# Value products of all attention heads in one run behind the last transpose, and tiles padded to 512 bytes

## The chip, the cores and the metric

The kernel runs on one core of a Trainium2 chip. The metric is the device time of one execution in microseconds (us), here as the median of several runs. TensorE (PE) multiplies matrices, VectorE (DVE) and ScalarE (ACT) work element by element, GpSimd (POOL) does small copies and memsets, and SyncE (SP) issues nearly all DMAs.

## The reference

A sequence of 512 tokens of width 1024 passes through two blocks, all in float32. The first block has two layers. Each layer runs two kinds of attention side by side, gates both and adds their output projection to x:

```
a = mla_attention(c_q, c_kv, k_r, ...) * silu(gate_a)      # 8 heads, all 512 keys, values 64 wide
b = dilated_attention(dil_qkv, ...) * silu(gate_b)         # 8 heads, 3 dilations, banded, mixed by their lse
x = x + concatenate([a, b], axis=-1) @ w_out[layer]
```

The second block has one layer: a SwiGLU FFN (2816 wide), a mixer, and a second FFN. The mixer adds two gated branches, a linear recurrent unit (RG-LRU) and a sliding-window attention with sinks and a relative bias (16 query heads, 4 key/value heads, 64 wide, windows of three chunks of 64).

In every attention the probabilities are normalised before they meet the values: o = (e / l) @ v.

## The kernel before, in words

**Products.** Activations stand transposed in SBUF, features on the partitions and the 512 tokens along the row. A projection keeps float32 precision by splitting each operand in a rounded high and a low part and taking three products (`mm3`, lines 131 to 133); for a width of 1024 a projection of 128 outputs is 24 products of 512 columns. `weights` loads one 128x1024 tile of weights, ACT writes its high part (`wh`) and DVE the low part (`wl`). These tiles come from the pools in `self.wps`, taken in turn: three times `wp`, and from the first FFN on one buffer of a pool `wx` besides.

**PSUM.** Its eight banks of 512 columns are given out in rings by purpose: `mm` for projections, `s` for scores, `t` for transposes, `o` for attention outputs.

**Order.** The kernel is written for a planner: each instruction has its place in the program as its priority, and the planner simulates the engines and gives each engine, which executes in order, the ready instruction of highest priority. So projections that stand later in the program fill the time in which attention waits for DVE and ACT. A dependency of the kind ORDER fixes only the order of two instructions on the same engine, without a semaphore; `begin` and `behind` make such dependencies.

**Latent attention** (`mla_attend`, 2 layers x 4 pairs of heads). For each of four query tiles r and two heads h: scores (lines 532 to 534), maximum, exponential, normalisation, four transposes into a `t` bank (`turn`, line 549), and one ACT copy of them to `PT` (line 550). `values(r)` then takes the eight products of the tile (line 558): the stationary operand is 64 columns of V, head 0 writes partitions 0 to 63 of the bank `o` and head 1 the other 64. Each such float32 product shows as two instructions in the trace. The loop calls `values(r)` two steps behind the transposes of the tile:

```
for i in range(8 + 1 + 2):
    ...
    i -= 1 + 2
    if i >= 0 and i % 2 == 1:
        values(i // 2)
```

**Dilated attention** (`dil_attend`, 2 layers x 4 pairs). The scores of all eight (tile, head) come first, then the factors that mix the dilations (lines 735 to 743). Then, tile by tile, DVE scales p (line 751), PE transposes (line 753), ACT copies (line 754), and eight products of the values follow (line 700, called through `add`).

**Sliding window** (`swa`, `swa_tile`, 4 groups of 4 query tiles). One call of `swa_tile` makes scores, softmax, transposes (line 1064), copies to `swPT` (three buffers, line 1066), the value products of the tile into half of bank 7 (line 1072: 4 instructions for the first tile, 8 for the others, each over 256 columns), and splits the output in high and low parts.

**Tiles.** Pools are laid out one behind the other in each partition of SBUF. `const` holds the vectors (178 columns, 712 bytes), the identity and a tile of ones; `wp`, `rows`, `xu` (x), `tmp`, `sm` (small vectors) follow, then the pools of the stages.

Of the kernel before, what the change touches and what calls it, by code (L numbers as in the profile page):

```python
# [11 lines left out]
F32 = mybir.dt.float32  # L12
# [10 lines left out]
P = 128  # L23
# [5 lines left out]
EPS = 1e-6  # L29
NEG = -1e30  # L30
GELU_C = 0.7978845608028654
SWAP32 = [i + 16 if i < 16 else i - 16 for i in range(32)]
SWAP16 = [i + 8 if i < 8 else i - 8 if i < 16 else i for i in range(32)]
WIN = (0, 16, 48, 64)
# [8 lines left out]
class Kern:  # L43
    def __init__(self, ctx, tc, a, out):
# [22 lines left out]
        self.ones = self.const.tile([P, P], F32, name="ones")  # L67
        nc.vector.memset(self.ones, 1.0)


    def banks(self, **kinds):

# [10 lines left out]
    def behind(self, ins, first):  # L83

        if first is None:
            return ins
        self.tc.add_manual_dep(ins, first.name, ORDER, reason="the bank's first product")
        return first

    def begin(self, ins, key, start):  # L90
# [233 lines left out]
class Block1:  # L324
# [195 lines left out]
    def mla_attend(self, L, pr, proj):  # L520
        k, nc, ap = self.k, self.k.nc, self.ap
        ve, mm = nc.vector, nc.tensor.matmul
        Q, Kh, Kl = proj
        V = self.VM[pr // 2]
        o = k.bank("o")
        ps, PT = [None] * 8, [None] * 4

        def softmax(r, h):
            c = slice(r * P, (r + 1) * P)
            qh, ql = Q[h]  # L530
            s = k.bank("s")
            mm(s, lhsT=qh[0:96, c], rhs=Kh[0:96, h, :], start=True, stop=False)  # L532
            mm(s, lhsT=qh[0:96, c], rhs=Kl[0:96, h, :], start=False, stop=False)  # L533
            mm(s, lhsT=ql[0:96, c], rhs=Kh[0:96, h, :], start=False, stop=True)  # L534
            mx, nm, l, rl = (k.small(n) for n in ("mx", "nm", "l", "rl"))
            ve.reduce_max(mx, s, axis=AX)
            ve.tensor_mul(nm, mx, self.msc[:, 4 + r:5 + r])
            p = ap.tile([P, S], F32, tag="p", name="p", bufs=8)
            nc.scalar.activation(p, s, AF.Exp, bias=nm, scale=self.msc[:, r:r + 1], accum_out=l)
            ve.reciprocal(rl, l)  # L540
            ve.tensor_scalar(p, p, rl, None, op0=ALU.mult)
            ps[2 * r + h] = p

        def turn(r, h):
            if h == 0:
                PT[r] = ap.tile([P, 2, 4, P], F32, tag="PT", name="PT", bufs=4)
            p, t = ps[2 * r + h], k.bank("t")
            for j in range(4):
                nc.tensor.transpose(t[:, j * P:(j + 1) * P], p[:, j * P:(j + 1) * P], k.ident)  # L549
            nc.scalar.copy(PT[r][:, h], t.rearrange("p (j q) -> p j q", j=4))  # L550

        def values(r):
            c = slice(r * P, (r + 1) * P)
            for j in range(4):
                for h in range(2):
                    vc = (j % 2) * 256 + (pr % 2) * P + 64 * h
                    b = slice(64 * h, 64 * h + 64)
                    k.begin(mm(o[b, c], lhsT=V[j // 2][:, vc:vc + 64], rhs=PT[r][:, h, j], start=j == 0, stop=j == 3),  # L558
                            (o.offset, h), j == 0)

        for i in range(8 + 1 + 2):
            if i < 8:
                softmax(i // 2, i % 2)
            if 0 <= i - 1 < 8:
                turn((i - 1) // 2, (i - 1) % 2)
            i -= 1 + 2
            if i >= 0 and i % 2 == 1:
                values(i // 2)
        self.gated(o, pr)

    def first_values(self, L):
# [119 lines left out]
    def dil_attend(self, L, pr, proj, V):  # L691
# [6 lines left out]
        def add(h, out, v, tile, pt, stop):  # L698
            vc = (tile % 2) * 256 + (pr % 2) * P + 64 * h
            ins = inst(mm(out[64 * h:64 * h + 64], lhsT=V[v][tile // 2][:, vc:vc + 64], rhs=pt,  # L700
                          start=(first[h] is None), stop=stop, skip_group_check=True))
            first[h] = k.behind(ins, first[h])


        own, oth, ps = k.small("own", 32, 2), k.small("oth", 32, 2), []
# [36 lines left out]
        ve.reciprocal(f, f)  # L742
        ve.tensor_mul(f, f, ev[:, 0])
        ov = by_tau(o)
        for n in range(4):
            PT = ap.tile([P, 2, 4, P], F32, tag="PT", name="PT", bufs=4)
            for h in range(2):
                p, t = ps[2 * n + h], k.bank("t")
                for i in range(2):
                    d = slice(256 * i, 256 * i + 256)  # L750
                    ve.tensor_scalar(p[:, d], p[:, d], fv[:, i, n, h:h + 1], None, op0=ALU.mult)
                for j in range(4):
                    nc.tensor.transpose(t[:, j * P:(j + 1) * P], p[:, j * P:(j + 1) * P], k.ident)  # L753
                nc.scalar.copy(PT[:, h], t.rearrange("p (j q) -> p j q", j=4))
            for j in range(4):
                for h in range(2):
                    if j < 2:
                        add(h, ov[:, n], 0, 2 * n + j, PT[:, h, j], False)
                    else:
                        add(h, o[:, n * P:(n + 1) * P], j - 1, n, PT[:, h, j], n == 3 and j == 3)  # L760
# [141 lines left out]
def mixer(k, acc, lead, hd, after, srcs):  # L902
# [3 lines left out]
    k.banks(mm=free[:2], t=(5, 6))  # L906
    rstd, R, first = k.start(acc, lead)
    with k.tc.tile_pool(name="mix", bufs=16, reuse_waits="tile") as mp:
        hb = mp.tile([P, 16], F32, name="hbg", bufs=1)
        o = a["voff"]["b_gate"]  # L910
        ve.tensor_scalar(hb, k.vecs[:, o:o + 16], 0.5, None, op0=ALU.mult)
        G = [None] * 16
# [42 lines left out]
def swa(k, R, rstd, at, gate, first):  # L955
    nc, a = k.nc, k.a
    ve, mm = nc.vector, nc.tensor.matmul
    with k.tc.tile_pool(name="swa", bufs=1, reuse_waits="tile") as sp:
# [38 lines left out]
        keys(0)  # L997
        Q = queries(0)
        keys(1)
        k.banks(mm=(0, 1, 2), s=(3, 4), t=(5, 6), o=(7,))  # L1000

        for g in range(4):
            bias = sp.tile([P, 4, 256], F32, tag="bias", name="bias", bufs=2)
            src = k.biases[4 * g:4 * g + 4]
            nc.sync.dma_start(bias, bass.AP(tensor=src.tensor, offset=src.offset + 127,
                                            ap=[[383, P], [384 * P, 4], [1, 256]]))
            nc.gpsimd.memset(bias[0:64, :, 192:256], NEG)
            nc.gpsimd.memset(bias[64:128, :, 0:64], NEG)
            for T in range(4):
                swa_tile(k, sp, g, T, Q, Kh[g], Kl[g], V, bias, at)  # L1010
            if g < 3:
                Q = queries(g + 1)
            for i in range(4):
                gate(4 * g + i)
# [12 lines left out]
    nc.sync.dma_start(k.biases, fb[0:16, None, :].to_broadcast([16, P, 384]))  # L1027


def swa_tile(k, sp, g, T, Q, Kh, Kl, V, bias, at):  # L1030

    nc = k.nc
    ve, mm = nc.vector, nc.tensor.matmul
# [3 lines left out]
    nk = len(kts)  # L1037
    n = nk * P
    kc = slice(base * P, base * P + 256)
    PT = sp.tile([P, 2, 4, P], F32, tag="swPT", name="swPT", bufs=3)  # L1040
    for hp in range(2):
        t = k.bank("t").rearrange("p (a b c) -> p a b c", a=2, b=2)
        s = k.bank("s", (2, 256))
        mx, nm, l, rl, es = (k.small(x, 2) for x in ("mx", "nm", "l", "rl", "es"))
        sk = k.vecs[:, k.a["voff"]["sinks"] + 4 * g + 2 * hp:][:, 0:2]
        p = sp.tile([P, 2, 256], F32, tag="swp", name="swp", bufs=2)
        for j in range(2):
            hl = 2 * hp + j
            mm(s[:, j], lhsT=Q[hl][:, c], rhs=Kh[:, kc], start=True, stop=False)
            mm(s[:, j], lhsT=Q[hl][:, c], rhs=Kl[:, kc], start=False, stop=True)  # L1050
            ve.tensor_tensor_reduce(out=p[:, j, 0:n], in0=s[:, j, 0:n], in1=bias[:, hl, 256 - n:256], scale=1.0,
                                    scalar=-3e38, op0=ALU.add, op1=ALU.max, accum_out=mx[:, j:j + 1])
        ve.tensor_tensor(mx, mx, sk, op=ALU.max)
        ve.tensor_scalar(nm, mx, -1.0, None, op0=ALU.mult)
        ve.tensor_sub(es, sk, mx)
        for j in range(2):
            nc.scalar.activation(p[:, j, 0:n], p[:, j, 0:n], AF.Exp, bias=nm[:, j:j + 1], accum_out=l[:, j:j + 1])
        nc.scalar.activation(es, es, AF.Exp)
        ve.tensor_add(l, l, es)
        ve.reciprocal(rl, l)  # L1060
        for j in range(2):
            ve.tensor_scalar(p[:, j, 0:n], p[:, j, 0:n], rl[:, j:j + 1], None, op0=ALU.mult)
            for i in range(nk):
                nc.tensor.transpose(t[:, i, j, :], p[:, j, i * P:(i + 1) * P], k.ident)
        for i in range(nk):
            nc.scalar.copy(PT[:, i, 2 * hp:2 * hp + 2, :], t[:, i])

    o = k.bank("o")[:, 0:256]
    for i, kt in enumerate(kts):
        pp = PT[:, i].rearrange("p (a b) q -> p b a q", b=2)  # L1070
        for j in range(2):
            mm(o[64 * j:64 * j + 64, :], lhsT=V[:, kt, g * 64:g * 64 + 64], rhs=pp[:, j], start=i == 0, stop=kt == T)
    for j in range(2):
        k.split(at[0][2 * g + j][:, c], at[1][2 * g + j][:, c], o[:, j * P:(j + 1) * P])


def lru(k, R, lr, other):
# [77 lines left out]
def tile_kernel(ctx, tc, a, out):  # L1155
# [21 lines left out]
                k.take_x(m, x, k.vcol(g, m), acc, part, sq)  # L1177
        return after

    k.wps = [*k.wps, ctx.enter_context(tc.tile_pool(name="wx", bufs=1))]  # L1180
    acc = ffn(k, *acc, 1, hd[0], to(hd[1], "mix_pre_g"), (a["w_k"][0], a["w_k"][1], a["w_q"][0], a["w_q"][1]))
    acc = mixer(k, *acc, hd[1], to(hd[2], "ffn2_pre_g"), up(2))
    ffn(k, *acc, 2, hd[2], to(out, None), ())
# [133 lines left out]
```

## Time and profile before

| | us |
|---|---|
| median of 3 runs | 2182.97 |
| lowest, highest | 2180.61, 2182.98 |
| profiled execution, its own time | 2184.09 |
| its span, first to last instruction | 2182.3 |
| PE busy in the span | 2145.0 |
| DVE, ACT, POOL busy | 1329.7, 965.1, 94.5 |

The profiled execution is one run more. Its span leaves out what lies before the first and behind the last instruction. Busy time of PE is modelled: a matmul is drawn from its start to the modelled end of its results, so that neighbours overlap.

### The profile page before, as it was taken

The numbers are of one execution on the slowest core, as the hardware profiler recorded it, in microseconds if no ns is written. First come the engines' busy times: TensorE is split into PE (matmuls) and PEld (weight loads), VectorE is DVE, ScalarE is ACT, GpSimd is POOL, SyncE is SP. The second block draws the span as 40 slices with busy tenths as digits, with TensorE's granted clock in tenths as the row PEclk, the third lists the DMA queues.
The fourth block names the chain that finished last, engine by engine and source line by source line (L and its number), as shares of the span: only waits on it lengthen the run. The fifth ranks groups of instructions, "written<-read, shape, count | busy, mean of one in ns | idle before, by whom it ended". The sixth has DMA issues, their size and how long they took to land.

```text
span 2182.3 us, 30506 instructions
## 1 busy us (share of the span) xinstructions
PE 2145.0 (98%) x11650; PEld 1773.3 (81%) x11650; DVE 1329.7 (61%) x2958; ACT 965.1 (44%) x1747; POOL 94.5 (4%) x350
## 2 busy tenths in 40 slices
PE   8999999999999999999999999999999999999997
PEld 7778779778788779778888888877788888888886
DVE  5866773765766773868555424966688748555323
ACT  5654443453653443545222223665567535222221
POOL 0000210100000210100000000000000000000001
PEclk9999999999999999999999999999999999999998
DMA  5313223383223333325223323322122425232221
GB/s 168 93 54 91 84 88 125 101 164 106 76 60 91 87 88 116 107 78 174 97 97 97 97 96 102 121 87 69 64 94 95 146 93 168 97 97 97 97 97 58
DMA packets 84690, 219.11 MB, mean 100 GB/s; under 512 B 9632, under 2 KB 29888, under 8 KB 84544
## 3 DMA queue, kind: packets, MB, share of 16 engines
q1 hardware_dynamic: 84544, 217.17, 32.4%
q8 instruction: 91, 1.49, 0.3%
q14 instruction: 55, 0.45, 0.1%
HBM read 190.92 MB, written 15.73 MB: 95 GB/s over the span
## 4 chain that ended last, share of the span: by engine, by line
PE 89%; DVE 5%; ACT 3%; DMA 2%; POOL 1%; issue 1%; SPq 0%; ACTq 0%; DVEq 0%
PE ps L131 24%; PE ps L132 24%; PE ps L133 24%; PE ps L157 4%; PE ps L700 2%; PE ps L558 2%; PE ps L753 2%; PE ps L549 1%; DVE wl L124 1%; POOL oth L645 1%; PE ps L716 1%; PE ps L532 1%; PE ps L534 1%; ACT p L724 1%; PE ps L533 1%
## 5 line engine op out<-in xcount | busy, mean ns | idle before, releaser
L122 ACT CAST wh<-wr 128x1024 fp32r<-128x1024 f32 (+3 forms) x338 | 342.7, 1015 | 735.5 <-PE ps L132 621.2
L131 PE MATMUL ps<-xh,wh 128*128 128x512 f32 x1496 | 589.5, 394 | 0.0
L132 PE MATMUL ps<-xl,wh 128*128 128x512 f32 x1496 | 589.0, 394 | 0.0
L133 PE MATMUL ps<-xh,wl 128*128 128x512 f32 x1496 | 588.8, 394 | 0.0
L124 DVE TENSOR_TENSOR wl<-wr,wh 128x1024 fp32r<-128x1024 f32 (+3 forms) x338 | 398.3, 1180 | 298.2 <-ACT wh L122 295.9
L133 PEld LDWEIGHTS ps<-xh,wl 128*128 128x128 f32 x1496 | 281.2, 188 | 59.0 <-issue 2.5
L131 PEld LDWEIGHTS ps<-xh,wh 128*128 128x128 f32 x1496 | 281.3, 188 | 58.8 <-issue 2.4
L132 PEld LDWEIGHTS ps<-xl,wh 128*128 128x128 f32 x1496 | 281.3, 188 | 57.0 <-issue 1.4
L131 PE MATMUL ps<-gh,wh 128*128 128x512 f32 (+1 forms) x540 | 199.8, 370 | 0.8 <-ACT wh L122 0.6
L132 PE MATMUL ps<-gl,wh 128*128 128x512 f32 (+1 forms) x540 | 199.0, 369 | 1.1 <-DVE gl L171 1.1
L133 PE MATMUL ps<-gh,wl 128*128 128x512 f32 (+1 forms) x540 | 197.5, 366 | 1.2 <-DVE wl L124 1.2
L133 PE MATMUL ps<-wh,xl 128*128 128x256 f32 (+1 forms) x416 | 119.3, 287 | 0.0
L132 PE MATMUL ps<-wl,xh 128*128 128x256 f32 (+1 forms) x416 | 119.3, 287 | 0.0
L131 PE MATMUL ps<-wh,xh 128*128 128x256 f32 (+1 forms) x416 | 118.9, 286 | 0.0
L131 PEld LDWEIGHTS ps<-gh,wh 128*128 128x128 f32 x540 | 101.5, 188 | 20.4 <-ACT wh L122 2.1
L133 PEld LDWEIGHTS ps<-gh,wl 128*128 128x128 f32 x540 | 101.5, 188 | 19.3 <-DVE wl L124 2.5
L132 PEld LDWEIGHTS ps<-gl,wh 128*128 128x128 f32 x540 | 101.6, 188 | 18.8 <-DVE gl L171 2.5
L853 DVE TENSOR_TENSOR x<-ps,R 128x512 f32<-128x512 f32 x44 | 30.4, 691 | 103.9 <-PE ps L133 103.9
L851 DVE TENSOR_TENSOR x<-ps,R 128x512 f32<-128x512 f32 x44 | 30.4, 691 | 85.8 <-PE ps L133 83.8
L132 PEld LDWEIGHTS ps<-wl,xh 128*128 128x128 f32 x416 | 79.4, 191 | 1.5 <-issue 1.0
L645 POOL COPY oth<-own 32x4 f32<-32x4 f32 x256 | 61.2, 239 | 442.1 <-ACT p L724 432.9
L133 PEld LDWEIGHTS ps<-wh,xl 128*128 128x128 f32 x416 | 79.4, 191 | 1.1 <-issue 1.0
(300 smaller groups left out, 3325.2 us busy)
## 6 DMA issues: line engine op xcount, KB each, us to landing
wr<-in_ffn_w SPq DMA_DIRECT2D x132, 512.0 KB, 3.5
wr<-in_w_dqk SPq DMA_DIRECT2D x48, 512.0 KB, 3.6
wr<-in_w_dv SPq DMA_DIRECT2D x20, 512.0 KB, 3.7
wr<-in_w_out SPq DMA_DIRECT2D x16, 512.0 KB, 3.6
wr<-in_w_bgate SPq DMA_DIRECT2D x16, 512.0 KB, 3.5
hd<-h SPq DMA_DIRECT2D x48, 128.0 KB, 1.8
h<-hd SPq DMA_DIRECT2D x24, 256.0 KB, 5.3
wr<-in_w_lat SPq DMA_DIRECT2D x10, 512.0 KB, 4.3
```

The lines of the kernel that those rows point to most:

```text
L122: nc.scalar.copy(hi[:, :cols], w[:, :cols])
L124: nc.vector.tensor_sub(lo[:, :cols], w[:, :cols], hi[:, :cols].bitcast(F32))
L131: first = mm(out, lhsT=wh, rhs=xh, start=start, stop=False)
L132: mm(out, lhsT=wh, rhs=xl, start=False, stop=False)
L133: return first, mm(out, lhsT=wl, rhs=xh, start=False, stop=stop)
L157: self.begin(mm(ps[:, part], lhsT=w[i][:, c], rhs=x[kt][:, part], start=start, stop=kt == KT - 1 and x is self.xl), ps.offset, start)
L558: k.begin(mm(o[b, c], lhsT=V[j // 2][:, vc:vc + 64], rhs=PT[r][:, h, j], start=j == 0, stop=j == 3), (o.offset, h), j == 0)
L645: self.mover.tensor_copy(dst[32 * b:32 * b + 32, a:a + 1], src[32 * a:32 * a + 32, b:b + 1])
L700: ins = inst(mm(out[64 * h:64 * h + 64], lhsT=V[v][tile // 2][:, vc:vc + 64], rhs=pt, start=(first[h] is None), stop=stop, skip_group_chec ...
L753: nc.tensor.transpose(t[:, j * P:(j + 1) * P], p[:, j * P:(j + 1) * P], k.ident)
L851: nc.vector.tensor_mul(x1, ps1, R)
L853: nc.vector.tensor_mul(x3, ps3, R)
```

## The change

In all three attentions the value products are issued behind the last transpose of their pair of heads (latent, dilated) or of their group (sliding window), and ORDER dependencies hold them there. In the sliding window, `swa_tile` now returns the turned weights, and a new function `swa_values` takes the products of four tiles and then splits the outputs. For that `swPT` has four buffers instead of three, the ring `o` two banks instead of one, and `mm` two instead of three.

Besides, unused tiles are added behind the tiles of `const` (160 bytes) and `sm` (448 bytes), and one small tile of the mixer is made 512 bytes wide; with `W_AT = 0` the other calls of `pad` add nothing. All pools then begin at multiples of 512 bytes.

```diff
+W_AT = 0
...
+        self.pad(self.const, 160 + W_AT)
+        self.pad(self.rows, 512 - W_AT)
+        self.pad(self.sm, 448)
+
+
+    def pad(self, pool, size):
+
+        if size % 512:
+            pool.tile([P, size // 4], F32, name="pad", tag="pad", bufs=1)
...
-                nc.tensor.transpose(t[:, j * P:(j + 1) * P], p[:, j * P:(j + 1) * P], k.ident)
+                turned[0] = inst(nc.tensor.transpose(t[:, j * P:(j + 1) * P], p[:, j * P:(j + 1) * P], k.ident))
...
-                    k.begin(mm(o[b, c], lhsT=V[j // 2][:, vc:vc + 64], rhs=PT[r][:, h, j], start=j == 0, stop=j == 3),
-                            (o.offset, h), j == 0)
-
-        for i in range(8 + 1 + 2):
+                    ins = mm(o[b, c], lhsT=V[j // 2][:, vc:vc + 64], rhs=PT[r][:, h, j], start=j == 0, stop=j == 3)
+                    k.begin(ins, (o.offset, h), j == 0)
+                    k.behind(inst(ins), turned[0])
+
+        for i in range(8 + 1):
             if i < 8:
                 softmax(i // 2, i % 2)
-            if 0 <= i - 1 < 8:
+            if i >= 1:
                 turn((i - 1) // 2, (i - 1) % 2)
-            i -= 1 + 2
-            if i >= 0 and i % 2 == 1:
-                values(i // 2)
+        for r in range(4):
+            values(r)
         self.gated(o, pr)
...
             first[h] = k.behind(ins, first[h])
+            k.behind(ins, turned)
...
-        for n in range(4):
-            PT = ap.tile([P, 2, 4, P], F32, tag="PT", name="PT", bufs=4)
+        PTs = [ap.tile([P, 2, 4, P], F32, tag="PT", name="PT", bufs=4) for n in range(4)]
+        for n, PT in enumerate(PTs):
...
+        for n, PT in enumerate(PTs):
             for j in range(4):
...
-        hb = mp.tile([P, 16], F32, name="hbg", bufs=1)
+        hb = mp.tile([P, P], F32, name="hbg", bufs=1)[:, 0:16]
...
-        k.banks(mm=(0, 1, 2), s=(3, 4), t=(5, 6), o=(7,))
+        k.banks(mm=(0, 1), s=(3, 4), t=(5, 6), o=(2, 7))
...
-            for T in range(4):
-                swa_tile(k, sp, g, T, Q, Kh[g], Kl[g], V, bias, at)
+            PTs = [swa_tile(k, sp, g, T, Q, Kh[g], Kl[g], bias) for T in range(4)]
+            swa_values(k, g, PTs, V, at)
...
-    PT = sp.tile([P, 2, 4, P], F32, tag="swPT", name="swPT", bufs=3)
+    PT = sp.tile([P, 2, 4, P], F32, tag="swPT", name="swPT", bufs=4)
...
+def swa_values(k, g, PTs, V, at):
+
+    mm = k.nc.tensor.matmul
+    os = [k.bank("o", (2, 256)) for _ in range(2)]
+    for T, (PT, _) in enumerate(PTs):
+        o = os[T // 2][:, T % 2]
+        kts = range(max(T - 1, 0), T + 1)
+        for i, kt in enumerate(kts):
+            pp = PT[:, i].rearrange("p (a b) q -> p b a q", b=2)
+            for j in range(2):
+                ins = mm(o[64 * j:64 * j + 64, :], lhsT=V[:, kt, g * 64:g * 64 + 64], rhs=pp[:, j], start=i == 0, stop=kt == T)
+                k.begin(ins, (os[T // 2].offset, j), i == 0)
+                k.behind(inst(ins), PTs[3][1])
+    for T in range(4):
+        c = slice(T * P, (T + 1) * P)
         for j in range(2):
...
+            k.split(at[0][2 * g + j][:, c], at[1][2 * g + j][:, c], os[T // 2][:, T % 2, j * P:(j + 1) * P])
```

## Rows read from the trace of the kernel before

**Rows 1.** The page: engines' busy time, and PE's granted clock in 40 slices.

```profile
PE 2145.0 (98%) x11650; PEld 1773.3 (81%) x11650; DVE 1329.7 (61%) x2958; ACT 965.1 (44%) x1747; POOL 94.5 (4%) x350
...
PEclk9999999999999999999999999999999999999998
```

**Rows 2.** The page: the chain that ended last, by engine.

```profile
PE 89%; DVE 5%; ACT 3%; DMA 2%; POOL 1%; issue 1%; SPq 0%; ACTq 0%; DVEq 0%
```

**Rows 3.** Timeline of PE, dilated stage: start us, us, engine, line, operands, count.

```profile
262.33 0.43 PE L700 MATMUL ps<-PT,V 128*64 128x128 f32 x2
262.70 0.50 PE L133 MATMUL ps<-xh,wl 128*128 128x512 f32 x1
263.03 0.39 PE L131 MATMUL ps<-xh,wh 128*128 128x512 f32 x1
263.26 0.40 PE L132 MATMUL ps<-xl,wh 128*128 128x512 f32 x1
263.59 1.09 PE L700 MATMUL ps<-PT,V 128*64 128x128 f32 x14
264.61 0.50 PE L133 MATMUL ps<-xh,wl 128*128 128x512 f32 x1
264.94 0.39 PE L131 MATMUL ps<-xh,wh 128*128 128x512 f32 x1
```

**Rows 4.** Timeline of PE: transposes in three stages, and a visit between them.

```profile
139.69 0.60 PE L549 MATMUL ps<-ident,p 128*128 128x128 f32 x4
...
257.59 0.66 PE L753 MATMUL ps<-ident,p 128*128 128x128 f32 x4
258.18 1.09 PE L700 MATMUL ps<-PT,V 128*64 128x128 f32 x14
259.19 0.66 PE L753 MATMUL ps<-ident,p 128*128 128x128 f32 x4
...
1405.69 0.27 PE L1064 MATMUL ps<-ident,swp 128*128 128x128 f32 x1
```

**Rows 5.** Timeline of PE, sliding-window stage.

```profile
1413.99 0.40 PE L133 MATMUL ps<-xh,wl 128*128 128x512 f32 x1
1414.31 1.08 PE L1072 MATMUL ps<-swPT,swV 128*64 128x256 f32 x8
...
1415.55 0.28 PE L1050 MATMUL ps<-swKl,swQ 128*128 128x256 f32 x1
```

**Rows 6.** Timeline of PE: first and last row of value products.

```profile
81.88 0.43 PE L558 MATMUL ps<-PT,VM 128*64 128x128 f32 x2
...
1560.39 1.08 PE L1072 MATMUL ps<-swPT,swV 128*64 128x256 f32 x8
```

**Rows 7.** Timeline of DVE and ACT in front of the dilated transposes.

```profile
252.89 4.30 DVE L751 TENSOR_SCALAR p<-p,f 128x256 f32<-128x256 f32 x16
...
254.03 1.26 ACT L754 COPY PT<-ps 128x512 f32<-128x512 f32 x2 [0.90 <-PE ps L753]
```

**Rows 8.** Waits of PE: us in total, times, longest.

```profile
PE ps L753 <- DVE p L751: 7.4, 8, 1.2
```

**Rows 9.** Windows, first latent pair and sliding window: busy us, clock, DMA.

```profile
77.00:98.00 21.00, 21.00 (x141) 15.20 (x140) 16.57 (x43) 14.41 (x30) 0.00 (x0) 1.00 0.14 39
...
1393.00:1430.00 37.00, 35.75 (x191) 26.60 (x191) 32.63 (x117) 27.86 (x80) 0.62 (x2) 1.00 0.28 86
```

**Rows 10.** Timeline of PE, first FFN: 24 products, then 72, first and last.

```profile
1017.61 0.40 PE L131 MATMUL ps<-xh,wh 128*128 128x512 f32 x1
...
1022.98 0.39 PE L133 MATMUL ps<-xh,wl 128*128 128x512 f32 x1
1023.21 0.39 PE L131 MATMUL ps<-xh,wh 128*128 128x512 f32 x1
...
1039.33 0.39 PE L133 MATMUL ps<-xh,wl 128*128 128x512 f32 x1
```

**Rows 11.** The page: line, engine, shapes, count, busy us, mean ns, idle before.

```profile
L131 PE MATMUL ps<-xh,wh 128*128 128x512 f32 x1496 | 589.5, 394 | 0.0
```

More of the change, by code (lines that the diff above doesn't have):

```diff
@@ L86, in behind @@
             return ins
-        self.tc.add_manual_dep(ins, first.name, ORDER, reason="the bank's first product")
+        self.tc.add_manual_dep(ins, first.name, ORDER, reason="behind it")
         return first
@@ L525, in mla_attend @@
         o = k.bank("o")
-        ps, PT = [None] * 8, [None] * 4
+        ps, PT, turned = [None] * 8, [None] * 4, [None]
         def softmax(r, h):
@@ L752, in dil_attend @@
                 for j in range(4):
-                    nc.tensor.transpose(t[:, j * P:(j + 1) * P], p[:, j * P:(j + 1) * P], k.ident)
+                    turned = inst(nc.tensor.transpose(t[:, j * P:(j + 1) * P], p[:, j * P:(j + 1) * P], k.ident))
                 nc.scalar.copy(PT[:, h], t.rearrange("p (j q) -> p j q", j=4))
+        for n, PT in enumerate(PTs):
             for j in range(4):
@@ L1027, in rel_biases, with swa_tile @@
     nc.sync.dma_start(k.biases, fb[0:16, None, :].to_broadcast([16, P, 384]))
-def swa_tile(k, sp, g, T, Q, Kh, Kl, V, bias, at):
+def swa_tile(k, sp, g, T, Q, Kh, Kl, bias):
     nc = k.nc
@@ L1063, in swa_tile @@
             for i in range(nk):
-                nc.tensor.transpose(t[:, i, j, :], p[:, j, i * P:(i + 1) * P], k.ident)
+                turned = inst(nc.tensor.transpose(t[:, i, j, :], p[:, j, i * P:(i + 1) * P], k.ident))
         for i in range(nk):
             nc.scalar.copy(PT[:, i, 2 * hp:2 * hp + 2, :], t[:, i])
-    o = k.bank("o")[:, 0:256]
-    for i, kt in enumerate(kts):
-        pp = PT[:, i].rearrange("p (a b) q -> p b a q", b=2)
+    return PT, turned
+def swa_values(k, g, PTs, V, at):
[12 more added lines that the diff above has]
+        c = slice(T * P, (T + 1) * P)
         for j in range(2):
-            mm(o[64 * j:64 * j + 64, :], lhsT=V[:, kt, g * 64:g * 64 + 64], rhs=pp[:, j], start=i == 0, stop=kt == T)
-    for j in range(2):
-        k.split(at[0][2 * g + j][:, c], at[1][2 * g + j][:, c], o[:, j * P:(j + 1) * P])
+            k.split(at[0][2 * g + j][:, c], at[1][2 * g + j][:, c], os[T // 2][:, T % 2, j * P:(j + 1) * P])
 def lru(k, R, lr, other):
@@ L1178, in to @@
         return after
-    k.wps = [*k.wps, ctx.enter_context(tc.tile_pool(name="wx", bufs=1))]
+    wx = ctx.enter_context(tc.tile_pool(name="wx", bufs=1))
+    k.wps = [*k.wps, wx]
+    k.pad(wx, W_AT)
+    if W_AT:
+        k.pad(ctx.enter_context(tc.tile_pool(name="wy", bufs=1)), 512 - W_AT)
     acc = ffn(k, *acc, 1, hd[0], to(hd[1], "mix_pre_g"), (a["w_k"][0], a["w_k"][1], a["w_q"][0], a["w_q"][1]))
```

## The prediction

> **What bounds the kernel now.** I read the page first. [...] "Busy" is not the whole reading, because ends of matmuls are modelled. What counts is the pitch, the time from one start to the next, and for this the timeline of PE alone is the view to read.
>
> There the reader should look at what happens where a value product (128x64 stationary, so half of the array's columns) stands next to anything that uses all 128 columns. Undisturbed 512-column products follow each other in 0.23 us (263.03 to 263.26). A visit of 14 value instructions lasts 1.02 us to the next start, one of 2 lasts 0.37 us, so twelve more cost 0.65 us, 0.054 us each [rows 3]. Now measure across a visit: from the product at 263.26 to the second one behind the visit at 264.94 are 1.68 us. In it are two full products (0.46) and 14 value instructions (0.76), together 1.22. So 0.46 us are spent on nothing but going into the narrow form and coming back. Between transposes it is a little less: transposes stand 0.11 us apart (four take 0.60, one alone 0.27, and the difference is three pitches), and 257.59 to 259.19 are 1.60 us for four of them (0.44) and 14 value instructions (0.76), which leaves 0.40 [rows 4]. In the sliding-window stage, 1413.99 to 1415.55 are 1.56 us for one 512-column product (0.23), eight value instructions of twice the columns (0.87 at twice 0.054) and one 256-column score product (0.12, half of a 512-column one), which leaves 0.34 [rows 5].
>
> How many visits there are is counted as rows of that timeline with line 558, 700 or 1072 between other rows: 66, 64 and 16, 146 in all, the first at 81.88 and the last at 1560.39 [rows 6]. 48 of those of line 700 stand between transposes on both sides. They are so many because the first product of a tile needs only head 0's copy and the rest also needs head 1's, so that the order on PE is 2, something else, 14.
>
> **The change, part by part.** *Value products behind the last transpose.* No product, transpose, copy or DMA is added or removed. Removed are entries and exits. Now: 48 x 0.40 + 82 x 0.46 + 16 x 0.34 = 19.2 + 37.7 + 5.4 = 62.3 us. After: one visit for each of 8 pairs of the latent stage, 8 pairs of the dilated stage and 4 groups of the window stage, 16 x 0.46 + 4 x 0.34 = 8.7 us. That is 53.6 us less, all on PE, the engine that sets the end. The value instructions themselves keep their 0.054 us.
>
> Is the run really unbroken? Its last quarter needs the copy of the last transposes. A copy is issued about 0.63 us after the one before it (two in 1.26) [rows 7]. Three quarters of a pair's run, 48 instructions, take 2.6 us, so that this copy has landed well before it is needed; I cost that wait at nothing. Without that cover it would be one copy, 0.6 us, in 20 places, 12 us. Were the planner to cut each pair's run once, 16 more visits would cost 7.4 us.
>
> *What takes the place of the value products among the transposes.* In the dilated stage a pair has 8 blocks of transposes, 3.5 us of PE. They are paced by DVE's scaling of p (16 in 4.30 us, 0.54 a block) and ACT's copies (0.63 a block, 5.0 us for 8) [rows 7]. Today value products fill the difference of 1.5 us. Later only projections of the next pair can. If they do, nothing is lost; if none does, 8 x 1.5 = 12 us. PE already waits in front of these blocks for DVE's p, 7.4 us in 8 places [rows 8], so the planner's idea of DVE is too rosy there. I take 4 us lost, nearer to full cover, since one 512-column product of 0.23 us fits each hole.
>
> *Four buffers for the turned weights at once* (window stage, from three) and all four of a dilated pair allocated ahead: the values that free them come before the next pair's transposes in the program, so nothing waits; cost nothing. The output evacuation (`gated`, `keep`, the splits) comes after the run, a few us later than for the first tile now; behind it lie the next projections. *Projection banks in the window stage fall from three to two* (bank 2 now holds outputs). One projection of 24 products takes 5.5 us (24 at 0.23), the bank behind it has that long to be read; DVE is busy 32.63 of 37 us there and PE idle 1.25 [rows 9]. I cost it at nothing, with 4 groups x 1 us as the upper bound.
>
> *Padding.* The pads put every pool at a multiple of 512 bytes. Before, the program places the weight buffers of pool `wp` and x at 352 beyond such a multiple, block-1 tiles, hidden rows and the weight buffer of pool `wx` at 416, mixer tiles at 480; the sizes of the pads undo just these (160 = 512 - 352; with 160 and 448, 416 becomes 1024). Does placement show? Yes: 24 products of one projection whose weights lie in `wx` start at 1017.61 and end their starts at 1022.98, 23 pitches of 233.5 ns; the next 72, weights and x both at 352, run from 1023.21 to 1039.33, 71 pitches of 227.0 ns [rows 10]. From the FFN on every fourth weight tile lies in `wx`; about 26 projections of x, 630 products, have the former placement, and at 6.5 ns each they give 4.1 us. Other pairings I leave at nothing, with plus or minus 4 us. [...]
>
> **Sum.** The profiled execution took 2184.09 us, 1.1 above the median shown, 2182.97. 2184.1 - 53.6 + 4 - 4.1 = 2130.4, and on the scale of the median 2129.
>
> **Rivals.** (a) *PE starves a little or the runs are cut*: full 12 us in the dilated blocks and 7.4 us of cuts, 2129 + 8 + 7 = 2144, up to 2165. For it: the waits of [rows 8]. Against: the many projections that follow at once.
>
> (b) *Placement is worth more.* Everything that PE reads lies today at an odd multiple of 32 bytes, so a true multiple of 64 or 512 was never seen. If it took another 6.5 ns off each of the 3 x 1,496 products of lines 131 to 133 that read x [rows 11], that is 29 us: 2100. For it: one placement step does cost that much. Against: nothing in the trace shows a pitch far below 227. [...]
>
> (c) *Slower: the attention stretches are paced by DVE and ACT, not by PE.* Then they keep their length when value products leave, PE idles there, and the runs are added behind: 16 x (64 x 0.054 + 0.46) = 63 us and some 13 for the window groups, 2184 + 76 = 2260 at worst. It decides from 3.4 us of new idle time a pair (53.6 / 16). For it: DVE 16.57 of 21 us busy in the first latent pair, 32.63 of 37 in the window stage [rows 9]. Against: PE is busy for all of the 21 us in that stretch, and the projections that now follow as a block can move in.
>
> (d) *The change does little*: other matmuls interleave with the run wherever the planner likes, and only placement remains, about 2179.
>
> **How the numbers follow.** Forecast, 2115 to 2142: 0.64. (a), 2142 to 2165: 0.15. (b), 2060 to 2115: 0.11. (d), 2165 to 2187: 0.05, of it 0.04 within 0.2% (4.4 us, about what a measurement of this kernel can tell from no change). (c), slower by more than that: 0.05. So faster 0.91, same 0.04, slower 0.05. The range 2108 to 2152 holds the forecast, about two thirds of (a) and a third of (b), near 0.8.
>
> **What would show it.** Rows of the value lines in PE's timeline should number about 20, each of 64 instructions (28 in the window stage) and some 3.5 us. The share of PE as an engine stays at 98% with the span shorter. PE's idle time before the dilated transposes should stay below 7.4 + 12 us. Projections with weights in `wx` should show 227 ns. The prediction is wrong if visits stay many, if PE idles over 3 us a pair, or if the pitch of all products moves by several ns either way.

## The result, and the profile after

The changed kernel takes 2133.57 us (median of 4 runs, 2133.02 to 2137.14), the kernel before 2182.1 beside it (4 runs). The ratio is 0.978 [0.977, 0.980], so 48.5 us are gone. The forecast was 2129, with a range of 2108 to 2152.

The page of the changed kernel, PE's busy time and clock, and the chain that ended last by engine:

```profile
PE 2093.3 (98%) x11650; PEld 1767.1 (83%) x11650; DVE 1329.9 (62%) x2958; ACT 958.9 (45%) x1747; POOL 94.9 (4%) x350
...
PEclk9999999999999999999999999999999999999999
...
PE 86%; DVE 7%; ACT 3%; POOL 2%; issue 1%; DMA 1%; SPq 0%; DVEq 0%; ACTq 0%
```

PE runs the same 11,650 instructions at the same granted clock (mean 0.997 before, 0.998 after), is busy 51.7 us less, and is still busy 98% of the span, which fell from 2182.3 to 2131.8 us [rows 1]. DVE's part of the chain rose from 5% to 7% [rows 2], a hint that not all of PE's gain was kept.

The timeline of PE in one dilated pair, then of DVE and of ACT there (start us, us, engine, line, operands, count, and the idle time before with what ended it). Lines have moved: the three products of a projection are L141 to L143 now, the value products L568 (latent), L710 (dilated) and L1092 (window), the transposes L559, L764 and L1076.

```profile
385.78 0.70 PE L764 MATMUL ps<-ident,p 128*128 128x128 f32 x4 [0.84 <-DVE p L762]
386.23 0.48 PE L143 MATMUL ps<-xh,wl 128*128 128x512 f32 x1
386.55 3.62 PE L764 MATMUL ps<-ident,p 128*128 128x128 f32 x28
390.10 3.71 PE L710 MATMUL ps<-PT,V 128*64 128x128 f32 x64
393.75 0.50 PE L141 MATMUL ps<-xh,wh 128*128 128x512 f32 x1
394.08 0.39 PE L142 MATMUL ps<-xl,wh 128*128 128x512 f32 x1
```

```profile
385.37 4.29 DVE L762 TENSOR_SCALAR p<-p,f 128x256 f32<-128x256 f32 x16
```

```profile
386.51 4.28 ACT L765 COPY PT<-ps 128x512 f32<-128x512 f32 x8 [1.15 <-PE ps L764]
```

Where [rows 3] had values and projections by turns, there is one row of 64 value products, 3.65 us to the next start, with nothing inside it. Over the whole trace the value lines make 20 such rows, 16 of 64 and 4 of 28. In front of it stand 28 transposes in a row, and these are not at their own pace. From 386.55 to 390.10 are 3.55 us. At 0.109 us each, and with 0.09 us for the step into the narrow form (from the last transpose to the first value product are 0.20 us), they would need 3.14. The 0.41 us over that fit the pace of what feeds and clears them: DVE gives a block of p every 0.54 us (16 instructions, 4.29 us, two a block), ACT copies a block every 0.535 us (8 in 4.28), and four transposes need only 0.44. Which of the two holds PE up these rows don't tell.

One window group of the changed kernel, PE's timeline:

```profile
1383.21 0.60 PE L1076 MATMUL ps<-ident,swp 128*128 128x128 f32 x4
1383.74 3.24 PE L1092 MATMUL ps<-swPT,swV 128*64 128x256 f32 x28
1386.91 0.50 PE L143 MATMUL ps<-xh,wl 128*128 128x512 f32 x1
1387.25 0.39 PE L141 MATMUL ps<-xh,wh 128*128 128x512 f32 x1
```

Four transposes (0.44), 28 products (28 x 0.108 = 3.02) and one full product (0.23) are 3.69 us; from 1383.21 to 1387.25 are 4.04. A visit still costs 0.35 us, near the 0.34 worked out from [rows 5], but there are four and not sixteen.

Taking the pitch (start to next start) of every PE instruction, less what its shape takes when undisturbed, and adding up around the visits, gives 61.8 us for the 146 visits of before and 7.0 for the 20 of after. That is 54.8 us gained, and the span shows 50.5. Placement gained several us besides (below), so that some 12 us were given back (54.8 and about 7.5, less 50.5). Three views say where. The waits of PE, changed kernel (what waited, for what: us in total, times, longest):

```profile
PE ps L764 <- DVE p L762: 7.4, 8, 1.2
...
PE ps L559 <- DVE p L551: 1.2, 3, 0.5
...
PE ps L542 <- ACT p L549: 0.8, 2, 0.4
```

then the window of the first latent pair (busy us of PE, PEld, DVE, ACT, POOL, granted clock, DMA):

```profile
77.00:98.00 21.00, 19.99 (x153) 15.63 (x151) 18.33 (x49) 15.23 (x33) 0.00 (x0) 1.00 0.22 64
```

and PE's timeline inside that window:

```profile
88.62 0.66 PE L559 MATMUL ps<-ident,p 128*128 128x128 f32 x4
89.65 0.50 PE L542 MATMUL ps<-KMh,qh 96*128 96x512 f32 x1 [0.37 <-ACT p L549]
```

The wait before the first dilated transposes is the same to the digit as in [rows 8]. New are waits of latent transposes (L559) for p, and of scores (L542) for the exponential (L549) that reads the scores before them out of their bank. In the window that [rows 9] showed with PE busy for all of 21.00 us, PE now idles 1.01, and DVE works 18.33 us where it worked 16.57 (the stage also starts 1.9 us sooner, so that the window holds a somewhat later stretch of it). Idle time is only part of such a wait: from 88.62 to 89.65 are 1.03 us for four transposes that need 0.44, so 0.59 us are lost where the row shows 0.37 idle, because the modelled end of the last transpose covers the rest.

### The profile page after: what moved, and what is told of

The parts are those of the page before. It is cut to its first block, busy times and chain, and to the rows that moved or that the text cites. A ratio compares the mean times of both kernels' runs of the same rounds, so it can differ in the third digit from the quotient of the medians.

```text
span 2131.8 us, 30572 instructions
## 1 busy us (share of the span) xinstructions
PE 2093.3 (98%) x11650; PEld 1767.1 (83%) x11650; DVE 1329.9 (62%) x2958; ACT 958.9 (45%) x1747; POOL 94.9 (4%) x350
## 3 DMA queue, kind: packets, MB, share of 16 engines
q1 hardware_dynamic: 84544, 217.17, 32.8%
## 4 chain that ended last, share of the span: by engine, by line
PE 86%; DVE 7%; ACT 3%; POOL 2%; issue 1%; DMA 1%; SPq 0%; DVEq 0%; ACTq 0%
PE ps L143 23%; PE ps L141 23%; PE ps L142 23%; PE ps L167 5%; PE ps L764 2%; PE ps L710 1%; PE ps L568 1%; DVE wl L134 1%; POOL oth L655 1%; PE ps L559 1%; PE ps L727 1%; ACT p L735 1%; PE ps L542 1%; PE ps L213 1%; PE ps L1092 1%
## 5 line engine op out<-in xcount | busy, mean ns | idle before, releaser
L141 PE MATMUL ps<-xh,wh 128*128 128x512 f32 x1496 | 587.3, 393 | 0.0
L143 PE MATMUL ps<-xh,wl 128*128 128x512 f32 x1496 | 587.1, 393 | 0.0
L143 PEld LDWEIGHTS ps<-xh,wl 128*128 128x128 f32 x1496 | 281.1, 188 | 56.9 <-issue 1.5
L141 PEld LDWEIGHTS ps<-xh,wh 128*128 128x128 f32 x1496 | 281.2, 188 | 56.4 <-issue 1.5
L142 PEld LDWEIGHTS ps<-xl,wh 128*128 128x128 f32 x1496 | 281.1, 188 | 54.8
L141 PE MATMUL ps<-gh,wh 128*128 128x512 f32 (+1 forms) x540 | 199.2, 369 | 1.3 <-ACT wh L132 1.2
L143 PE MATMUL ps<-gh,wl 128*128 128x512 f32 (+1 forms) x540 | 198.1, 368 | 1.9 <-DVE wl L134 1.2
L141 PE MATMUL ps<-wh,xh 128*128 128x256 f32 (+1 forms) x416 | 119.0, 286 | 0.0
L143 PE MATMUL ps<-wh,xl 128*128 128x256 f32 (+1 forms) x416 | 118.9, 286 | 0.0
L141 PEld LDWEIGHTS ps<-gh,wh 128*128 128x128 f32 x540 | 101.9, 189 | 20.2 <-ACT wh L132 2.6
L142 PEld LDWEIGHTS ps<-gl,wh 128*128 128x128 f32 x540 | 101.8, 189 | 18.8 <-DVE gl L181 2.2
L143 PEld LDWEIGHTS ps<-gh,wl 128*128 128x128 f32 x540 | 101.8, 189 | 18.4 <-DVE wl L134 2.5
L141 PEld LDWEIGHTS ps<-wh,xh 128*128 128x128 f32 x416 | 79.5, 191 | 0.6
```

Source lines behind the costliest of these rows:

```text
L141: first = mm(out, lhsT=wh, rhs=xh, start=start, stop=False)
L142: mm(out, lhsT=wh, rhs=xl, start=False, stop=False)
L143: return first, mm(out, lhsT=wl, rhs=xh, start=False, stop=stop)
```

## The experiments

Each time is a median, each ratio is to the kernel before on the same chip (2180.55, 2180.95 and 2181.53 us in the three groups: the first four, the next four, the last three).

**Order alone, and placement alone.** The first is the changed kernel without its pads, the second the kernel before with them.

```diff
-        self.pad(self.const, 160 + W_AT)
-        self.pad(self.rows, 512 - W_AT)
-        self.pad(self.sm, 448)
...
-        hb = mp.tile([P, P], F32, name="hbg", bufs=1)[:, 0:16]
+        hb = mp.tile([P, 16], F32, name="hbg", bufs=1)
```

> The new order of the value products without any padding (pools where they were in the kernel before). If visits to the narrow form are the cause (0.36 to 0.46 us each, 126 fewer), nearly all of the gain stays: 2138 to 2141 us, 42 to 45 less than before. If placement were the cause, about 2175 to 2180.

> The padding alone, with the order of before. If visits are the cause and only the offset between weights and moving operand matters, 4 to 8 us less than before: 2175 to 2179. If placement carried the gain, about 2140.

Order alone: 2143.39 us, 0.983 [0.982, 0.985], so 37 us, less than expected. Placement alone: 2172.72, 0.996 [0.995, 0.998], so 8 us, the upper end of what was expected. The two parts add up to 45, near the whole (48.5). Order is worth some 12 us less than the forecast's 49.6 (53.6 less 4), placement about twice its 4.1. In the trace of order alone the visits are 20 and the time around them is as low as in the changed kernel, so what is missing was lost elsewhere.

**What placement acts on.** One kernel moves all weight tiles by 64 bytes against the data that they multiply; the other moves everything behind `const` by 32 bytes, weights and data alike.

```diff
-W_AT = 0
+W_AT = 64
```

```diff
-        self.pad(self.const, 160 + W_AT)
+        self.pad(self.const, 192 + W_AT)
```

> The changed kernel with all weight buffers 64 bytes beyond the multiple of 512 at which everything else stands. If the offset between the moving operand and the weights sets the pitch, all 512-column products of projections go from 227 to about 233.5 ns, as those with weights in wx did before: some 6,600 x 6.5 ns = 43 us more, less about 9 us for 2,100 256-column products that get faster, so 2163 to 2172. If TensorE's two reads never meet, no change from the changed kernel: 2134.

> The changed kernel with all pools 32 bytes beyond a multiple of 512, together. If only the offset between the two operands matters, no change: 2134. If a true multiple of 64 or 512 is what helps, the pitch of all products moves; at 6.5 ns for 4,500 to 6,600 products 29 to 43 us more.

Weights moved: 2164.61 us, 0.993 [0.991, 0.994], 31 us slower than the changed kernel. All moved: 2138.48, 0.981 [0.979, 0.982], some 5 us slower, with an interval that just overlaps that of the changed kernel. The first FFN shows the pitch. First and last product of a stretch of one shape, the changed kernel, then weights moved, then all moved:

```profile
984.73 0.39 PE L142 MATMUL ps<-xl,wh 128*128 128x512 f32 x1
...
1039.13 0.39 PE L142 MATMUL ps<-xl,wh 128*128 128x512 f32 x1
```

```profile
984.82 0.39 PE L142 MATMUL ps<-xl,wh 128*128 128x512 f32 x1
...
1035.22 0.39 PE L142 MATMUL ps<-xl,wh 128*128 128x512 f32 x1
```

```profile
984.69 0.39 PE L141 MATMUL ps<-xh,wh 128*128 128x512 f32 x1
...
1039.09 0.39 PE L141 MATMUL ps<-xh,wh 128*128 128x512 f32 x1
```

240 pitches in 54.40 us are 226.7 ns; 216 in 50.40 are 233.3; 240 in 54.40 are 226.7 again. So the distance between the weights and the moving data counts, and not where both lie, in the three places seen: at a multiple of 512, 32 bytes beyond one, and 352 beyond one (227.0 in [rows 10]). Rival (b) of the prediction, which needed a true multiple of 64 or 512, falls, and no stretch of these products goes below 226.6 ns either. The 5 us of the kernel with all moved are not in the pitch; its waits for weight tiles and row statistics are longer (L141 for wh 2.8 us in all against 1.2, L222 for rstd 4.7 against 3.4), and why is open.

**Each attention stage alone** (the kernel before, with the edit of one stage).

```diff
# latent alone
-        for i in range(8 + 1 + 2):
+        for i in range(8 + 1):
...
+        for r in range(4):
+            values(r)
# dilated alone
+            k.behind(ins, turned)
...
+        for n, PT in enumerate(PTs):
```

> Only the latent stage has its value products in one run per pair; everything else, placement too, as before. 58 visits fewer. If PE bounds the latent stage, 58 x 0.45 = 26 us less than before: about 2156. If DVE and ACT set part of its pace, PE waits more and some 6 to 8 us of it are given back: about 2163.

> Only the dilated stage has its value products in one run per pair; everything else as before. 56 visits fewer, 24 us; the transposes then wait for DVE's scaling, about 4 us: 20 us less than before, 2162. If these waits are not real losses, 2158; if the stage were paced by DVE, no gain, 2182.

Latent alone: 2165.51 us, 0.993 [0.991, 0.995]. That is 15.4 us where its visits give 26 in the trace, so some 10 us of the gain are given back there. Dilated alone: 2163.09, 0.992 [0.990, 0.993], 17.9 us, near what was expected with the transposes' wait in the sum.

**Is it the 64-column form?** The kernel before, in its own order, but each value product takes all 128 columns of the pair's V, and both heads are added into each other: what it computes is another thing, with the same count of instructions, again in 146 groups on PE.

```diff
-                    k.begin(mm(o[b, c], lhsT=V[j // 2][:, vc:vc + 64], rhs=PT[r][:, h, j], start=j == 0, stop=j == 3),
-                            (o.offset, h), j == 0)
+                    k.begin(mm(o[:, c], lhsT=V[j // 2][:, vc - 64 * h:vc - 64 * h + 128], rhs=PT[r][:, h, j], start=j == 0 and h == 0, stop=j == 3 and h == 1),
+                            (o.offset, 0), j == 0 and h == 0)
```

> The order of before, but every value product of the latent and dilated stages takes 128 columns of V and writes all 128 partitions, both heads added into each other, so the output is another one. If the 64-column form is what costs, the rows across a visit lose their 0.40 to 0.46 us (under 0.1 left) in 130 visits, 54 us less, while the 1,024 instructions cost about 0.110 instead of 0.054 us, 57 us more: about the time of before, 2180 to 2190. If the float32 form after the rounded one is what costs (or the waits at a visit), the excess stays and the time is about 2240.

It took 2194.64 us, 1.006 [1.005, 1.008], 5 us over the range expected if the form is what costs, and far from the other. PE's timeline there, a visit of 14:

```profile
265.69 0.40 PE L132 MATMUL ps<-xl,wh 128*128 128x512 f32 x1
265.93 1.75 PE L700 MATMUL ps<-PT,V 128*128 128x128 f32 x14
267.43 0.48 PE L133 MATMUL ps<-xh,wl 128*128 128x512 f32 x1
267.75 0.40 PE L131 MATMUL ps<-xh,wh 128*128 128x512 f32 x1
```

From 265.69 to 267.75 are 2.06 us. Two full products (0.46) and 14 products at twice the pitch (0.109, 1.53) are 1.99. So 0.07 us go to the visit, where [rows 3] show 0.46. Over the 130 latent and dilated visits it is 0.1 us on average; the window visits, left in the narrow form, keep 0.36. The total fell from 61.8 to 17.7 us, 44 less, and the wider products cost more than that: 1,024 of them at 0.055 us more are 56. The price of a visit is for the greatest part that of changing between 128x64 and 128x128.

**A run for each query tile** (the changed kernel with the run cut in four, and head 1 first, so that each part is unbroken; all pads kept).

```diff
-                turned[0] = inst(nc.tensor.transpose(
+                turned[r] = inst(nc.tensor.transpose(
...
-                for h in range(2):
+                for h in (1, 0):
...
-        for r in range(4):
-            values(r)
+            i -= 1 + 2
+            if i >= 0 and i % 2 == 1:
+                values(i // 2)
```

> The changed kernel, with a run per query tile instead of one per pair in the latent and dilated stages (head 1 before head 0, so that a tile is not cut): 74 visits in the planned order, 54 more than in the changed kernel. If each visit costs 0.36 to 0.46 us, 19 to 25 us more, less up to 7 us of waits that the value products cover again: 2146 to 2158. If what helped was anything else, 2134.

It took 2144.61 us, 0.983 [0.982, 0.984], 11 us more than the changed kernel and just under the range expected. It makes 74 visits, and the time around visits rises from 7.0 to 25.7 us, by 18.7. So 7 to 8 us came back somewhere. Its window of the first latent pair:

```profile
77.00:98.00 21.00, 20.88 (x155) 16.00 (x154) 19.14 (x50) 15.63 (x34) 0.00 (x0) 1.00 0.21 64
```

PE idles 0.12 us there and not 1.01, and the waits of the latent transposes for p are gone from its list. To see such waits whole, take all of PE's pitches from the first to the last score or transpose of the stage, leave out those around visits, and take off one undisturbed pitch a shape (227 ns for 512 columns, 120 for 256, 110 for a transpose, 234 for a score product of 96 rows). What is left in the latent stage is 3.0 us in the kernel before, 12.7 in the changed one, 12.6 with latent alone, and 4.6 here. Value products between the transposes were cover for late inputs of PE.

**Late for what?** Is it DVE's scaling of p by the row sums that the transposes wait for? The scaling of the latent and the dilated stage is left out, in the changed kernel and in the kernel before, so neither normalises its weights.

```diff
-            ve.tensor_scalar(p, p, rl, None, op0=ALU.mult)
...
-                for i in range(2):
-                    d = slice(256 * i, 256 * i + 256)
-                    ve.tensor_scalar(p[:, d], p[:, d], fv[:, i, n, h:h + 1], None, op0=ALU.mult)
```

> The changed kernel without the VectorE instructions that multiply the weights p by one over the row sum (latent and dilated attention; 8 of 512 columns and 16 of 256 a pair), so its values are not normalised. Theory: some 11 us of what the runs gained are given back in the two attention stages, because the transposes, now in a row, wait for VectorE's p. Without that work some 6 to 11 us come back: 2123 to 2128, and the 28 transposes of a dilated pair either fall from 0.53 to 0.44 us a block, or, if ScalarE's copies (0.535 us a block) are as much the pace, stay at 0.53. Rival: the difference between the 54.8 us that left the visits and the 50.5 us that left the span is spread over weight waits and the planner's order and has nothing to do with VectorE: 2131 to 2135.

> The kernel before without the same instructions. Theory (the value products in between covered VectorE's pace before): it gains less than the changed kernel does by the same edit, at most the 7.4 us that the dilated transposes waited for p, so 2175 to 2181, and the distance between this kernel and the changed one without them is 51 to 56 us, the full worth of the visits and the placement. Rival: the distance stays at the 48.6 us that the two kernels with the scaling have.

Changed without scaling: 2127.73 us, 0.975 [0.974, 0.976], 6 us less, which by itself lies at the edge of the theory's range. Before without scaling: 2173.04, 0.996 [0.995, 0.998], 8.5 less, where the theory allowed it 7.4 at most and less than the changed kernel gains. The transposes of a dilated pair don't stand in a row of 28 there, so that their pace can't be compared. The distance between the two is 45.3 us, not 51 to 56. Part of that is a shift of the order itself: without the scaling the kernel before makes 132 visits (57.5 us), not 146. Corrected for these 4.3 us it is 49.6, the rival's 48.6 within what can be told. Both also got one long wait for a weight tile, 6.7 and 8.7 us, where the scaled kernels wait 1.2 and 0.6 at that line (waits of PE, changed without scaling, then before without scaling):

```profile
PE ps L141 <- ACT wh L132: 6.7, 1, 6.7
```

```profile
PE ps L131 <- ACT wh L122: 8.7, 1, 8.7
```

So the theory in this form falls: DVE's scaling is not what the change added. Added up as above, the lost time of the latent and dilated stages together goes from 18.8 to 31.9 us by the change with the scaling, and from 6.3 to 19.0 without it, 13 us more each time. In the latent stage alone leaving it out takes 12.7 to 7.9 us in the changed kernel, 3.0 to 1.5 in the kernel before.

**A version that might have gained.** Part of the scaling goes to GpSimd: head 1's p in the latent stage, the last two blocks of a dilated pair.

```diff
-            ve.tensor_scalar(p, p, rl, None, op0=ALU.mult)
+            (nc.gpsimd if h else ve).tensor_scalar(p, p, rl, None, op0=ALU.mult)
...
-                    ve.tensor_scalar(p[:, d], p[:, d], fv[:, i, n, h:h + 1], None, op0=ALU.mult)
+                    (nc.gpsimd if n == 3 else ve).tensor_scalar(p[:, d], p[:, d], fv[:, i, n, h:h + 1], None, op0=ALU.mult)
```

> The changed kernel with part of that scaling on GpSimd: head 1's p in the latent stage, and the last two of eight blocks of a dilated pair. Theory (VectorE paces the transposes): 2128 to 2132, if GpSimd is quick enough; its addition of 256 columns took 0.80 us, by which a p of 512 takes at most some 1.6 us and would be ready later than VectorE's, which is the case against it. Rival: no gain, 2133 to 2145, because head 1's p is late by a microsecond or the two engines get in each other's way.

It took 2171.82 us, 0.995 [0.994, 0.997]: 38 us slower than the changed kernel, far beyond both expectations. The groups of GpSimd (count, busy us, mean ns of one) and the first wait of PE:

```profile
L551 POOL TENSOR_SCALAR p<-p,rl 128x512 f32<-128x512 f32 x32 | 51.8, 1617 | 250.2 <-DVE rl L550 168.1 <-PE ps L544 42.7 <-PE ps L143 20.8
L762 POOL TENSOR_SCALAR p<-p,f 128x256 f32<-128x256 f32 x32 | 30.8, 975 | 27.9 <-DVE f L754 27.9
```

```profile
PE ps L559 <- POOL p L551: 28.2, 28, 1.5
```

1.62 us for one p is what the addition had foretold, and 28 of the 32 made PE wait, 28.2 us in all, 1.0 each: other products did not cover a p that late. Added up as above, the latent stage loses 38.7 us where the changed kernel loses 12.7, and the dilated stage 32.8 where it loses 19.2. None of the runs that normalise the weights beats the changed kernel.

## Why the prediction was right

**The visits** were the right mechanism at the right price: 146 became 20, and 54.8 us left them against 53.6 in the sum. The full-width run shows the cause: one way in and out of the narrow form costs 0.34 to 0.46 us, and with products of 128 columns a visit costs 0.1 us on average.

**The run is unbroken**, 20 rows of 64 and 28, and the wait on its last copy costs nothing that the trace shows, as costed.

**The dilated transposes** were costed at 4 us, because DVE (0.54 us a block) and ACT (0.63) were taken to pace them. The row of 28 shows 0.41 us, which for 8 pairs is 3.3 in all, and the wait in front is unchanged at 7.4. No projection filled the holes, contrary to the reason given for taking 4 and not 12; it stayed small because a hole is 0.07 us (0.41 over the six steps between seven blocks), not the 0.19 that ACT's 0.63 less 0.44 gives. ACT's copy, taken as 0.63 us, runs at 0.535 when the blocks follow each other.

**The latent stage is the term that the sum lacked.** Of rival (c) I had argued that PE is busy for all of 21 us in the first latent pair. True, but the value products were part of what kept it busy. The lost time there rose by 9.7 us (3.0 to 12.7), 1.2 a pair: rival (c) in kind, far from the 3.4 us a pair from which it decides. The run for each query tile shows the other side of it, the lost time back at 4.6 us and its added visits dearer than that.

**Placement was mis-sized**, 4.1 us against 8 measured alone. The step "other pairings I leave at nothing" failed. By sums of pitches, before against after: first products of the FFNs 439.7 to 436.0 us, 512-column outputs 211.1 to 209.4, the recurrent branch's projections 143.1 to 141.4, the output projection of the window attention 44.9 to 43.9; the 256-column outputs went the other way, 54.5 to 55.5. If placement made no difference, the run with moved weights would equal the changed kernel; it is 31 us slower.

**The sum again.** Counted in the way described at the run for each query tile, all of PE's pitches can be given to one of five places (us over the undisturbed pitch; with this yardstick the visits come to 61.4 and 6.8 us, not 61.8 and 7.0):

| | visits | latent | dilated | window | all else |
|---|---|---|---|---|---|
| kernel before | 61.4 | 3.0 | 15.8 | 6.3 | 28.0 |
| order alone | 6.8 | 12.7 | 18.9 | 8.1 | 28.1 |
| changed kernel | 6.8 | 12.7 | 19.2 | 7.1 | 19.0 |

Order alone takes 54.6 us from the visits and gives back 9.7, 3.1 and 1.8, so that 40.0 are left, and its span is 41.1 us shorter. The pads then take another 9.8, in the placement named above and in some waits, and its span is 9.4 us shorter again. The forecast took 4 us to be given back where it was 14.6, and 4.1 for placement where it was 8 to 10. The two errors have opposite signs and in part cancelled, so that it is luck that the total came within 5 us. Which engine is late for the latent transposes is open: it is not the scaling alone.

## What to carry to other kernels

Count the changes of form on PE (half of the columns, then all) in the timeline and price one from two starts around it; grouping such products was worth 0.34 to 0.46 us here for each visit saved, before what comes back as waits (some 10 of 26 us in the latent stage). Before taking filler from between dependent steps, see what those steps' inputs are paced by: an engine that reads as busy all the time may be busy because of that filler (PE in the first latent pair: 21.00 of 21 us with it, 19.99 without). Compare the places of weights and of the data streamed against them: weights moved by 64 bytes took the products of 512 columns from 226.7 to 233.3 ns here, and made the kernel 31 us slower.

## What was not expected of the hardware

In these runs the pitch of back-to-back products goes with the distance between the moving operand and the weights, both taken as remainders to 512 bytes, as the pads are sized; that 512 and no other size is the measure was not shown. For 512 columns of the rounded parts it is 226.7 ns where both have the same place, about 229 where the moving operand lies 64 bytes further, and 233 where it lies 128 further or 64 less far (the kernel before, by the addresses in its program, and for the last the run with moved weights). Other distances were not run. For 256 columns the sign turns: in the outputs of the FFNs the mean is 121 ns at the same place and 116 in the run with moved weights. In that run 512-column FFN products went from 436.0 to 448.6 us, while 256-column outputs fell from 55.5 to 53.2 and the dilated values' from 117.6 to 115.7. Why is not settled by these runs.
